# A decoder block with two recurrent mixers: another prologue and DeltaNet preparation, sigmoid gates inside the second recurrence, held joins, six steps a chunk

## The chip, the cores and the metric

The kernel runs on one core of a Trainium2 chip. The metric is the time of one execution in microseconds (us), the median of several runs. Engines: PE (TensorE, matrix products), DVE (VectorE), ACT (ScalarE), POOL (GpSimd), and SP, whose queue starts all DMA transfers of this kernel. Every engine works through its own list of instructions in order; semaphores tie them together.

## The reference

One block on x of 512 positions by 1024 channels, float32. A conditioning vector c gives shift, scale and gate by adaLN: a product of silu(c) with a 1024 x 6144 matrix. The normed and modulated x goes through one wide projection w_in to all inputs of two mixers and to two gates:

```python
h = rms_norm(x) * (1 + scale) + shift
q, k, v = split(silu(causal_conv4(h @ w_qkv)))         # gated DeltaNet, 8 heads of 64
y_gdn  = rms_norm(delta_rule(l2(q), l2(k), v, g, beta)) * silu(h @ w_z)
y_rwkv = group_norm(rwkv7_scan(r, decay, k, v, -kk, kk * a)) + bonus, times a gate
x = x + gate * ((sigmoid(ga) * (y_gdn @ w_bg) + sigmoid(gb) * (y_rwkv @ w_br)) @ w_out)
x = x + gate2 * conv_glu(rms_norm(x) * (1 + scale2) + shift2)      # 1024 -> 2 x 2816 -> 1024
```

Both recurrences run in 8 chunks of 64 positions; within a chunk a unit triangular 64 x 64 matrix per head is inverted.

## The kernel before, in words

**Layout.** All activations are kept as [channel, time], 128 channels by 512 positions a tile. A product tile of w_in takes 8 steps (k) of 3 matmuls: high part of the weights by high part of h (L187), high by low (L190), low by high (L191), all fp32r, 24 matmuls in a row into one of two PSUM banks (`mm`). The weights come as one 512 KB transfer into `raw`; ACT makes the high part `whi` (L146), DVE the low part `wlo` (L149). bg and br tiles have half the depth, 12 matmuls.

**Queue.** Products wait in a Python list; `fill(n)` emits n steps at a place in the program, so that PE has something to do between the dependent pieces of the recurrences; `need` emits until a product is done. When a product is begun, the weights of the next are requested. `late` adds transfers and sums of adaLN rows (`wada`, L210 and L211) ahead of a product. The framework's scheduler then orders each engine's instructions by what it thinks is ready, so the order isn't that of the program. Two things bind it: data, and `last["hold"]`, which puts every queue matmul behind the last `step` matmul that stands before it in the program (L188).

**Prologue (L333 to L371).** silu(c) is worked out on 128 x 8 numbers, spread to all partitions by two PE products. `first_tiles` does seven w_in tiles at once, k by k: two adaLN rows each summed on DVE (L202), A1 (L366), the normed h in high and low part (L305 to L307), the weights' low part on POOL for k from 1 on.

**DeltaNet preparation (L410 to L627).** Convolutions (one on ACT and POOL, L414 to L418, the others on DVE, L385), l2 norms (squares on POOL, L483), decay matrices (L505 on POOL, mask L512 on DVE), and a loop over chunks that makes `ginv`, the triangular matrices (L622 to L627).

**Solve (L541).** The 64 x 64 matrices are split in 32 x 32 blocks. They are written to DRAM (`lsc`, L548) and read back with another partition order (L551). DVE inverts the 32 x 32 blocks by 30 pairs of operations (L559, L561), ACT makes a transposed copy (`pr`, L565), and `tsc`, `usc` go through DRAM back. Then PE joins the blocks: for each half, 32 small matmuls (L582), a copy, 32 more (L592), a copy. It is a generator: the part after `yield` comes when it is run to its end, at L678 for DeltaNet (g) and at L850 for RWKV (r).

**Recurrences.** DeltaNet at L739 with 1, 1 and 3 steps of queue work (`more`) a chunk; RWKV at L856 with 3, 3 and 2 steps a chunk, `hold` on in both. Between them the pair matrices of RWKV (L807), its solve, the output norm of DeltaNet, silu(z), the eight bg products (into `ysc`) and transposes (`to_natural`). The order of queue products is GQ, LO, GV, RK and RR in turn, RV, Z, then gates GA (8) and GB (8), raw gates being copied to DRAM (`asc`, `bsc`).

**Merge (L936).** After the RWKV norm all of the queue is drained; the eight br products follow, each with two loads of gates, one of `ysc`, two sigmoids, a multiply on POOL (L944) and DVE work; then w_out, and the FFN.

Of the kernel before, what the change touches and what calls it, by code (L numbers as in the profile page):

```python
# [22 lines left out]
D = 1024  # L23
# [32 lines left out]
def body(ctx, tc, io, out, tap=lambda name, ap: None):  # L56
# [143 lines left out]
    def ada(j, w):  # L200
        sp.dma_start(w, io["w_ada"][j])
        i = dve.tensor_tensor_reduce(out=w, in0=w, in1=cond, scale=1.0, scalar=col("b_ada", j), op0=ALU.mult,  # L202
                                 op1=ALU.add, accum_out=mod[:, j:j + 1])
        if last["norm"] is not None:
            tc.add_manual_dep(i.ins, last["norm"].ins.name, after, reason="place")
# [20 lines left out]
    def product(label, src, xs_, evac, psum=mm, late=0, halves=False, spare=None):  # L226
# [3 lines left out]
        return dict(label=label, pieces=pieces, n=n, xs=xs_, evac=evac, psum=psum, late=late, halves=halves)  # L230

    def stream():
        while queue:
            it = queue.pop(0)
            for _ in range(min(it["late"], len(ada_rest))):
# [97 lines left out]
    cond = const.tile([128, D], F32, name="cond")  # L333
    table(EXP)
    fn(sc_, cc, AF.Exp, scale=-1.0)
    dve.tensor_scalar(sc_, sc_, 1.0, None, op0=ALU.add)
    dve.reciprocal(sc_, sc_)
    dve.tensor_tensor(sc_, sc_, cc, op=ALU.mult)
    pool.affine_select(out=diag.rearrange("p (k t) -> p k t", k=KT), in_=sc_.unsqueeze(2).broadcast_to([128, KT, 128]),
                       pattern=[[0, KT], [-1, 128]], base=0, channel_multiplier=1, compare_op=ALU.is_equal, fill=0.0)  # L340
    for u in range(2):
        p = pc()
        pe.matmul(p, one, diag[:, T * u:T * u + T], start=True, stop=True)
        act.copy(cond[:, T * u:T * u + T], p)
# [16 lines left out]

    def first_h(k):
        w = slot((2, 3, 8, 9, 12)[k]) if k < 5 else slot2((0, 2, 1)[k - 5])
        ada(8 + k, w[:, 0:D])
        ada(k, w[:, D:2 * D])
        dve.scalar_tensor_tensor(A1[:, k:k + 1], mod[:, 8 + k:9 + k], 1.0, col("norm1", k),  # L366
                                 op0=ALU.add, op1=ALU.mult)
# [42 lines left out]
    def gkq(a, j, side=False):  # L410
        def f(p):
            acc, w = tmp("sg" if side else "acc"), col("conv_gdn", 4 * (4 * (1 - a) + j), 4)
            if side:
                act.activation(acc, p, AF.Copy, scale=w[:, 3:4])  # L414
                for i in range(1, 4):
                    t = tmp("sp")
                    act.activation(t[:, :T - i], p[:, :T - i], AF.Copy, scale=w[:, 3 - i:4 - i])
                    pool.tensor_tensor(acc[:, i:], acc[:, i:], t[:, :T - i], op=ALU.add)  # L418
            else:
                conv(acc, p, w, 4)  # L420
# [82 lines left out]
    for b in range(4):  # L503
        gt = tmp("acc").rearrange("p (c h t) -> p c h t", c=2, h=4)
        pool.tensor_tensor(gt, gl[:, 2 * b:2 * b + 2, :].unsqueeze(3).broadcast_to([128, 2, 4, C]),  # L505
# [6 lines left out]
        dve.tensor_tensor(ex, ex, mask2[:, 1, :].unsqueeze(1).unsqueeze(1).broadcast_to([128, 2, 4, C]), op=ALU.mult)  # L512
# [28 lines left out]
    def solve(sv, name, work):  # L541
# [32 lines left out]
        yield  # L574
        for h in range(2):
# [3 lines left out]
            for i in range(16):  # L579
                for e in range(2):  # L580
                    lo_r, hi_r = slice(64 * e, 64 * e + 32), slice(64 * e + 32, 64 * e + 64)
                    pe.matmul(p[hi_r, i, :], sv[lo_r, 16 * h + i, 32:64], t1[lo_r, 16 * h + i, :],  # L582
# [6 lines left out]
            for i in range(16):  # L589
                for e in range(2):  # L590
                    lo_r, hi_r = slice(64 * e, 64 * e + 32), slice(64 * e + 32, 64 * e + 64)
                    pe.matmul(p[lo_r, i, :], ht[hi_r, i, :], sv[hi_r, 16 * h + i, 32:64],  # L592
                              start=True, stop=True)
# [23 lines left out]
    qs = [qe, ct4(gs[:, 2048:4096])]  # L617
    for c in range(NC):
# [5 lines left out]
        pool.tensor_tensor(qs[1][hs(1), :, tc_], qe[hs(1), :, tc_], eg[hs(1), :, tc_], op=ALU.mult)  # L624
# [19 lines left out]
    to_natural(gv, lambda e, c: gvn[hs(1 - e), c])  # L644
# [3 lines left out]
    zsc = dr.tile([4, 128, T], F32, name="zsc")  # L648
# [184 lines left out]
    for ct in range(4):  # L833
# [4 lines left out]
        split(ga_h[ct], ga_l[ct], sg)  # L838
    gx = list(zip(ga_h, ga_l))
# [9 lines left out]
    to_natural(kh, lambda e, c: kb[e][hs(1 - e), :, c * C:(c + 1) * C], True)  # L849
# [6 lines left out]
    for c in range(NC):  # L856
# [7 lines left out]
        fill(3)  # L864
# [5 lines left out]
        fill(3)  # L870
# [34 lines left out]
    table(EXP)  # L905
    rb_h, rb_l = quarter(slot(2, F32R)), quarter(slot(12, F32R))
# [22 lines left out]
    drain()  # L929
# [3 lines left out]
    mh = [hp.tile([128, T], F32R, name=f"hh{k}", tag=f"hh{k}") for k in range(KT)]  # L933
    ml = [hp.tile([128, T], F32R, name=f"hl{k}", tag=f"hl{k}") for k in range(KT)]

    def merge(n):  # L936
        def f(p):
            t, sa_t, sb_t, ya_t = tmp("acc"), tmp("sg"), tmp("sq"), tmp("rs")
            sp.dma_start(sa_t, asc[n])
            sp.dma_start(sb_t, bsc[n])  # L940
            sp.dma_start(ya_t, ysc[n])
            fn(sa_t, sa_t, AF.Sigmoid)
            fn(sb_t, sb_t, AF.Sigmoid)
            pool.tensor_tensor(ya_t, sa_t, ya_t, op=ALU.mult)  # L944
            dve.tensor_tensor(t, sb_t, p, op=ALU.mult)
            dve.tensor_tensor(t, t, ya_t, op=ALU.add)
            split(mh[n], ml[n], t)
        return f
# [211 lines left out]
```

## Time and profile before

| what | us |
|---|---|
| median of 3 runs (942.07 to 944.73) | 943.73 |
| the profiled execution, whole | 943.86 |
| its span of instructions | 942.2 |
| PE busy in the span | 887.0 |
| DVE / ACT / POOL busy | 548.0 / 413.5 / 150.0 |
| DeltaNet recurrence, first matmul | 208.66 |
| RWKV recurrence, first chunk's second step | 385.40 |
| FFN, from about | 565 |

How to read the profile: times are from the start of the span. A busy share is that of a stage; a row of the timeline gives start, length, engine, line, operation, output <- input and shape, and in brackets how long the engine had stood idle and what ended it. "xN" is the number of instructions in a row. PE matmuls overlap: a row's length is longer than the distance to the next.

### The profile page before, as it was taken

To read this page: it belongs to the slowest core of one execution; us is meant where nothing else is said; L and a number is where in the kernel's file an instruction comes from. 1 tells how busy PE (TensorE), PEld (TensorE's weight loads), DVE (VectorE), ACT (ScalarE), POOL (GpSimd) and SP (SyncE) were. 2 spreads that over 40 slices of the span, in tenths; PEclk is the share of its full clock that TensorE was granted. 3 is DMA by queue.
4 is the path that set the end of the run, shared out by engine and by line. 5 is a ranking of instruction groups with operands and counts; after the bars stand their busy time and mean duration, and the time that the engine had idled before them with its cause. 6 is when DMAs were issued, how large, how long until landed. Compare 5 with 4: busy or idle time off the path is not lost.

```text
span 942.2 us, 13945 instructions
## 1 busy us (share of the span) xinstructions
PE 887.0 (94%) x5463; PEld 690.9 (73%) x5463; DVE 548.0 (58%) x865; ACT 413.5 (44%) x663; POOL 150.0 (16%) x126
## 2 busy tenths in 40 slices
PE   5989889989989998899999999999999999999996
PEld 3666566876666776777667788888888888888885
DVE  7988988934976684245568537464544544322233
ACT  5247535355537658323465425343333333332231
POOL 2334630001542100011232230000000000010112
PEclk7999989989999999799999999999999999999998
DMA  9741232473234577444567543332232233533322
GB/s 322 261 151 46 67 101 68 144 170 102 58 90 112 197 232 202 142 146 153 186 200 256 181 139 91 106 106 96 90 103 99 89 105 97 173 101 100 96 89 90
DMA packets 81696, 126.26 MB, mean 134 GB/s; under 512 B 26237, under 2 KB 43005, under 8 KB 81566
## 3 DMA queue, kind: packets, MB, share of 16 engines
q1 hardware_dynamic: 81630, 125.36, 42.4%
q8 instruction: 43, 0.70, 0.3%
q14 instruction: 23, 0.19, 0.1%
HBM read 110.14 MB, written 14.68 MB: 132 GB/s over the span
## 4 chain that ended last, share of the span: by engine, by line
PE 70%; DVE 14%; ACT 7%; DMA 3%; issue 3%; POOL 2%; SPq 0%; DVEq 0%; ACTq 0%; POOLq 0%
PE ps_mm L187 19%; PE ps_mm L191 19%; PE ps_mm L190 19%; PE ps_pc L182 3%; DVE wlo L149 2%; ACT whi L146 1%; DVE slot L202 1%; ACT slot L607 1%; DMA wada<-in_w_ada 1%; DVE slotd L202 1%; DVE wada L211 1%; PE ps_pa L592 1%; ACT tmp_rs L94 1%; PE ps_pc L187 1%; PE ps_pa L622 1%
## 5 line engine op out<-in xcount | busy, mean ns | idle before, releaser
L187 PE MATMUL ps_mm<-hh,whi 128*128 128x512 f32 (+1 forms) x714 | 292.1, 410 | 8.5 <-ACT hh L306 3.5
L191 PE MATMUL ps_mm<-hh,wlo 128*128 128x512 f32 (+1 forms) x714 | 282.5, 396 | 4.7 <-POOL wlo L149 3.5
L190 PE MATMUL ps_mm<-hl,whi 128*128 128x512 f32 (+1 forms) x714 | 282.3, 395 | 1.5 <-DVE hl L307 1.5
L149 DVE TENSOR_TENSOR wlo<-raw,whi 128x1024 fp32r<-128x1024 f32 (+2 forms) x133 | 156.7, 1178 | 169.1 <-ACT whi L146 163.5
L146 ACT CAST whi<-raw 128x1024 fp32r<-128x1024 f32 (+2 forms) x140 | 136.9, 979 | 242.8 <-PE ps_mm L190 190.4
L187 PEld LDWEIGHTS ps_mm<-hh,whi 128*128 128x128 f32 x714 | 136.0, 191 | 47.6 <-issue 9.8
L191 PEld LDWEIGHTS ps_mm<-hh,wlo 128*128 128x128 f32 x714 | 136.6, 191 | 37.9 <-POOL wlo L149 5.2
L190 PEld LDWEIGHTS ps_mm<-hl,whi 128*128 128x128 f32 x714 | 136.7, 191 | 32.1 <-issue 3.6
L191 PE MATMUL ps_mm<-slot,wlo 128*128 128x512 f32 (+1 forms) x154 | 58.5, 380 | 1.7 <-DVE wlo L149 1.7
L187 PE MATMUL ps_mm<-slot,whi 128*128 128x512 f32 (+1 forms) x154 | 58.0, 379 | 0.0
L190 PE MATMUL ps_mm<-slot,whi 128*128 128x512 f32 (+1 forms) x122 | 45.4, 372 | 0.0
L968 POOL COPY tmp_rs<-tmp_sq 128x512 f32<-128x512 f32 x2 | 2.1, 1066 | 268.8 <-ACT tmp_sq L965 268.8
L211 DVE CUSTOM_DVE_ANT_0 wada<-wada,cond,cols 128x512 f32<-128x512 f32 x32 | 25.1, 785 | 26.5 <-DMA wada<-in_w_ada 26.3
L211 DVE CUSTOM_DVE_ANT_0 wada<-wada,cond,half 128x512 f32<-128x512 f32 x32 | 25.2, 787 | 21.7 <-DMA wada<-in_w_ada 21.6
L187 PE MATMUL ps_mm<-slotd,whi 128*128 128x512 f32 (+1 forms) x96 | 36.4, 379 | 0.0
L190 PE MATMUL ps_mm<-slotd,whi 128*128 128x512 f32 (+1 forms) x96 | 36.1, 376 | 0.0
L191 PE MATMUL ps_mm<-slotd,wlo 128*128 128x512 f32 (+1 forms) x96 | 36.1, 376 | 0.0
L970 POOL TENSOR_TENSOR tmp_rs<-tmp_rs,tmp_sq 128x512 f32<-128x512 f32 x12 | 19.5, 1624 | 103.8 <-ACT tmp_sq L965 103.8
L191 PEld LDWEIGHTS ps_mm<-slot,wlo 128*128 128x128 f32 x154 | 29.0, 188 | 9.1 <-DVE wlo L149 4.0
L1035 DVE TENSOR_TENSOR tmp_sg<-tmp_acc,ps_mm 128x512 f32<-128x512 f32 x20 | 13.8, 688 | 35.6 <-PE ps_mm L191 35.5
L385 DVE SCALAR_TENSOR_TENSOR tmp_acc<-ps_mm,cols,tmp_acc 128x511 f32<-128x511 f32 (+2 forms) x44 | 32.8, 745 | 0.7
L187 PEld LDWEIGHTS ps_mm<-slot,whi 128*128 128x128 f32 x154 | 28.9, 188 | 5.8 <-ACT whi L146 0.4
(279 smaller groups left out, 1336.0 us busy)
## 6 DMA issues: line engine op xcount, KB each, us to landing
raw<-in_w_in SPq DMA_DIRECT2D x40, 512.0 KB, 3.5
raw<-in_w_fi SPq DMA_DIRECT2D x37, 512.0 KB, 3.5
wada<-in_w_ada SPq DMA_DIRECT2D x64, 256.0 KB, 3.1
raw<-in_w_fo SPq DMA_DIRECT2D x16, 512.0 KB, 3.5
slot<-in_w_ada SPq DMA_DIRECT2D x10, 512.0 KB, 6.8
slot<-in_xT SPq DMA_DIRECT2D x16, 256.0 KB, 4.1
raw<-in_w_out SPq DMA_DIRECT2D x8, 512.0 KB, 3.7
raw<-in_w_in SPq DMA_DIRECT2D x8, 448.0 KB, 4.5
```

What stands on the lines that cost most here:

```text
L94: i = act.activation(*a, **k)
L146: i = act.copy(hi, src)
L149: j = eng.tensor_tensor(lo, src, hi.bitcast(F32), op=ALU.subtract)
L182: last["step"] = pe.matmul(*a, **k)
L187: i = pe.matmul(p, hi, xh, start=start, stop=False)
L190: pe.matmul(p, hi, xl, start=False, stop=False)
L191: pe.matmul(p, lo, xh, start=False, stop=stop)
L202: i = dve.tensor_tensor_reduce(out=w, in0=w, in1=cond, scale=1.0, scalar=col("b_ada", j), op0=ALU.mult, op1=ALU.add, accum_out=mod[:, j:j ...
L211: i = dve.tensor_tensor_reduce(out=w, in0=w, in1=cond[:, part], scale=1.0, scalar=half[:, j:j + 1] if u else col("b_ada", j), op0=ALU.mult ...
L385: dve.scalar_tensor_tensor(acc[:, i:], p[:, :T - i], w[:, taps - 1 - i:taps - i], acc[:, i:], op0=ALU.mult, op1=ALU.add)
L970: pool.tensor_tensor(sums[0], sums[0], sq, op=ALU.add)
L1035: dve.tensor_tensor(t, accs[j], p, op=ALU.mult)
```

## The change

It has six parts.

1. *Conditioning vector.* c comes as a 128 x 1024 broadcast from the host (512 KB), in the queue between the fourth and fifth tile of x; ACT takes its SiLU. The PE broadcast goes.
2. *Prologue.* Loads are requested one or two k ahead; the weights' low part is on DVE for all k; A1 on ACT.
3. *Preparation.* The one convolution goes to DVE; squares of the l2 norm go to ACT (L492 after), decay product (L514) to DVE, the mask to POOL as eight `affine_select`; `qs[1]` is one DVE operation ahead of the chunk loop; two fill steps a norm instead of one; copies of two transposes on ACT. The four Z products stand ahead of GV in the queue.
4. *Held joins.* Matmuls of the joins are `step`s and `hold` is on while they are emitted.
5. *Gates.* From ahead of the bg products ACT has the sigmoid table; a gate product is evacuated by sigmoid, GA multiplied by its y (fetched from DRAM). GB 6 and 7 are left for the branch stage, one ahead of br 0 and one ahead of br 3, and stay in SBUF; loads for the merge are requested one product ahead; `late` is 3 for GA, 4 for GB, 0 for br.
6. *RWKV recurrence.* Two, two and two queue steps a chunk.

```diff
-    sp.dma_start(cc, io["c"])
     for k in range(KT):
         sp.dma_start(xT(k), io["xT"][k])
+        if k == 3:
+            sp.dma_start(cond, io["c"])
...
-            split(hi[:, :128 * count], lo[:, :128 * count], raw[:, :128 * count], side if k else dve, () if k else behind)
+            split(hi[:, :128 * count], lo[:, :128 * count], raw[:, :128 * count], dve, () if k else behind)
...
+    table(SILU)
+    fn(cond, cond, AF.Silu)
     table(EXP)
-    fn(sc_, cc, AF.Exp, scale=-1.0)
...
-        dve.scalar_tensor_tensor(A1[:, k:k + 1], mod[:, 8 + k:9 + k], 1.0, col("norm1", k),
-                                 op0=ALU.add, op1=ALU.mult)
+        act.activation(A1[:, k:k + 1], mod[:, 8 + k:9 + k], AF.Identity, scale=col("norm1", k), bias=col("norm1", k))
...
+    for j in range(4):
+        inproj(T_Z + j, spill(zsc[j]))
     for j in range(4):
         inproj(T_GV + j, lambda p, j=j: conv(gv[:, j], p, col("conv_gdn", 4 * (8 + j), 4), 4))
...
-        pool.tensor_tensor(sq, dst, dst, op=ALU.mult)
+        act.activation(sq, dst, AF.Square)
...
-        pool.tensor_tensor(gt, gl[:, 2 * b:2 * b + 2, :].unsqueeze(3).broadcast_to([128, 2, 4, C]),
+        dve.tensor_tensor(gt, gl[:, 2 * b:2 * b + 2, :].unsqueeze(3).broadcast_to([128, 2, 4, C]),
...
-        dve.tensor_tensor(ex, ex, mask2[:, 1, :].unsqueeze(1).unsqueeze(1).broadcast_to([128, 2, 4, C]), op=ALU.mult)
+        for e in range(2):
+            d = ex[64 * e:64 * e + 64]
+            pool.affine_select(out=d, in_=d, pattern=[[0, 2], [0, 4], [1, C]], base=0, channel_multiplier=-1,
+                               compare_op=ALU.is_ge, fill=0.0)
...
+        held, last["hold"] = last["hold"], True
         for h in range(2):
...
-                    pe.matmul(p[hi_r, i, :], sv[lo_r, 16 * h + i, 32:64], t1[lo_r, 16 * h + i, :],
+                    step(p[hi_r, i, :], sv[lo_r, 16 * h + i, 32:64], t1[lo_r, 16 * h + i, :],
...
+    dve.tensor_tensor(qs[1][hs(1)], qe[hs(1)], eg[hs(1)], op=ALU.mult)
...
-        pool.tensor_tensor(qs[1][hs(1), :, tc_], qe[hs(1), :, tc_], eg[hs(1), :, tc_], op=ALU.mult)
...
+    def gate(n, dst):
+        def f(p):
+            o = tmp("sp")
+            if sig_in[0]:
+                fn(o, p, AF.Sigmoid)
+            else:
+                act.copy(o, p)
+                raw_gate.add(n)
+            if ("y", n) in fetched:
+                dve.tensor_tensor(o, o, fetched.pop(("y", n)), op=ALU.mult)
+                with_y.add(n)
+            sp.dma_start(dst, o)
+        return f
...
-        fill(3)
+        fill(2)
...
-    drain()
+    need(T_GB + KT - 3)
...
-            pool.tensor_tensor(ya_t, sa_t, ya_t, op=ALU.mult)
...
+        if n in (0, 3):
+            g = KT - 2 + n // 3
+            queue.append(product(T_GB + g, io["w_in"][T_GB + g], hx, last_gate(g), ahead=1))
-        queue.append(product(("br", n), io["w_br"][n], bx, merge(n), late=2))
+        queue.append(product(("br", n), io["w_br"][n], bx, merge(n), begin=merge_in(n), ahead=1))
```

How instructions move, on PE at the joins of the first solve. Before, from the last matmuls of the product `ps_mm_1652` (one of RK and RR; five whole ones of these stand right ahead of it) to the recurrence's first matmuls (`ps_pc_1684`); `slot10` and `slotd2` hold the solve's blocks:

```order
L187 MATMUL ps_mm_1652<-hh7_113,whi_1615 128x512
L190 MATMUL ps_mm_1652<-hl7_121,whi_1615 128x512
L191 MATMUL ps_mm_1652<-hh7_113,wlo_1616 128x512
L582 MATMUL ps_pa_1298<-slot10_943,slotd2_830 32x32 x31
L592 MATMUL ps_pa_1342<-slotd2_830,tmp_sg_1299 32x32
L582 MATMUL ps_pa_1390<-slot10_943,slotd2_830 32x32 x32
L592 MATMUL ps_pa_1432<-slotd2_830,tmp_sg_1391 32x32
L592 MATMUL ps_pa_1342<-slotd2_830,tmp_sg_1299 32x32 x31
L592 MATMUL ps_pa_1432<-slotd2_830,tmp_sg_1391 32x32 x31
L182 MATMUL ps_pc_1684<-slot8_1206,slotd2_830 64x64 x8
L690 MATMUL ps_pa_1697<-slot11_473 128x512
L187 MATMUL ps_mm_1706<-hh0_106,whi_1648 128x512
```

The joins follow the products and run without queue matmuls between them. The same place after, where `ps_mm_1376` is the first of the eight RK and RR products and the joins have L181, the line of `step`:

```order
L713 MATMUL ps_pa_1398<-slot11_461 128x512
L713 MATMUL ps_pa_1404<-slot11_461 128x512
L181 MATMUL ps_pa_1410<-slot10_957,slotd2_851 32x32 x32
L186 MATMUL ps_mm_1376<-hh6_110,whi_1366 128x512
L189 MATMUL ps_mm_1376<-hl6_118,whi_1366 128x512
L190 MATMUL ps_mm_1376<-hh6_110,wlo_1367 128x512
L186 MATMUL ps_mm_1376<-hh7_111,whi_1366 128x512
L189 MATMUL ps_mm_1376<-hl7_119,whi_1366 128x512
L190 MATMUL ps_mm_1376<-hh7_111,wlo_1367 128x512
L181 MATMUL ps_pa_1454<-slotd2_851,tmp_sg_1411 32x32 x32
L186 MATMUL ps_mm_1493<-hh0_104,whi_1372 128x512
L189 MATMUL ps_mm_1493<-hl0_112,whi_1372 128x512
```

The joins now come behind three quarters of the first RK product, two queue steps stand in each gap, and the rest of the RK and RR products follow behind the last join.

On SP at the first solve's write and read. Before:

```order
L548 DMA lsc_g_936<-slotd2_830 32x32x32 x4
L157 DMA raw_1252<-in_w_in 128x1024
L157 DMA raw_1258<-in_w_in 128x1024
L551 DMA slot10_943<-lsc_g_936 128x1024
L210 DMA wada_3039<-in_w_ada 128x512
```

After, with the spills of Z 0 to Z 3 (`zsc`):

```order
L409 DMA zsc_467<-tmp_sp_848 128x512
L560 DMA lsc_g_950<-slotd2_851 32x32x32 x4
L409 DMA zsc_467<-tmp_sp_1108 128x512
L409 DMA zsc_467<-tmp_sp_1142 128x512
L156 DMA raw_1145<-in_w_in 128x1024
L563 DMA slot10_957<-lsc_g_950 128x1024
L409 DMA zsc_467<-tmp_sp_1176 128x512
```

Two spills and one weight load stand between write and read where there were two weight loads.

More of the change, by code (lines that the diff above doesn't have):

```diff
@@ L224, in body, with product @@
     queue, done = [], set()
-    def product(label, src, xs_, evac, psum=mm, late=0, halves=False, spare=None):
+    def product(label, src, xs_, evac, psum=mm, late=0, halves=False, spare=None, begin=None, ahead=0):
         n = src.shape[-1] // 128
@@ L229, in product @@
                   for k0 in range(0, n, 8)]
-        return dict(label=label, pieces=pieces, n=n, xs=xs_, evac=evac, psum=psum, late=late, halves=halves)
+        return dict(label=label, pieces=pieces, n=n, xs=xs_, evac=evac, psum=psum, late=late, halves=halves, begin=begin, ahead=ahead)
     def stream():
@@ L234, in stream @@
             it = queue.pop(0)
+            for nx in [it] + queue[:it["ahead"]]:
+                if nx["begin"] is not None:
+                    nx["begin"]()
+                    nx["begin"] = None
             for _ in range(min(it["late"], len(ada_rest))):
@@ L408, in body, with gkq @@
     pool.memset(wt[64:65], 1.0)
-    def gkq(a, j, side=False):
+    def gkq(a, j):
         def f(p):
[L412 to L420, printed above, removed]
+            acc, w = tmp("acc"), col("conv_gdn", 4 * (4 * (1 - a) + j), 4)
+            conv(acc, p, w, 4)
             fn(kq[:, a, j], acc, AF.Silu)
         return f
-    inproj(T_GQ + 2, gkq(1, 2, True), pa)
+    inproj(T_GQ + 2, gkq(1, 2), pa)
     inproj(T_GQ + 3, gkq(1, 3))
@@ L597, in solve @@
                 act.mul(sv[lo_r, i_, 32:64], p[lo_r], -1.0)
+        last["hold"] = held
     def to_natural(src, place, quiet=False):
@@ L661, in body, with fetch, f @@
         shift_in(T_RV + j, rv_[:, j], 8 + j)
-    for j in range(4):
-        inproj(T_Z + j, spill(zsc[j]))
+    sig_in = [False]
+    raw_gate, with_y = set(), set()
+    fetched = {}
+    def fetch(label, tag, src):
+        def f():
+            fetched[label] = tmp(tag)
+            sp.dma_start(fetched[label], src)
+        return f
[11 more added lines that the diff above has]
+            sp.dma_start(dst, o)
+        return f
     for n in range(KT):
-        inproj(T_GA + n, spill(asc[n]))
-    for n in range(KT):
-        inproj(T_GB + n, spill(bsc[n]))
+        inproj(T_GA + n, gate(("a", n), asc[n]),
+               begin=lambda n=n: fetch(("y", ("a", n)), "rs", ysc[n])() if ("bg", n) in done else None)
+    for n in range(KT - 2):
+        inproj(T_GB + n, gate(("b", n), bsc[n]))
     lw = ct4(slot(12))
@@ L838, in body @@
         split(ga_h[ct], ga_l[ct], sg)
+    table(SIG)
+    sig_in[0] = True
     gx = list(zip(ga_h, ga_l))
@@ L928, in body, with last_gate, f, merge_in @@
         fill(2)
[L929 removed]
+    need(T_GB + KT - 3)
     table(SIG)
[L933 to L934 removed]
+    mh = quarter(slot(8, F32R)) + quarter(slot(10, F32R))
+    mls = slot2(0, F32R)
+    ml = [mls[:, T * k:T * k + T] for k in range(KT)]
+    gates, gate_slot = {}, quarter(slot(11))
+    def last_gate(n):
+        def f(p):
+            gates[n] = gate_slot[len(gates)]
+            fn(gates[n], p, AF.Sigmoid)
+        return f
     def merge(n):
         def f(p):
[L938 to L943, printed above, removed]
[L944 to L947 removed]
+            t = tmp("acc")
+            if n in gates:
+                sb_t = gates[n]
+            else:
+                sb_t = fetched[("b", n)]
+                if ("b", n) in raw_gate:
+                    fn(sb_t, sb_t, AF.Sigmoid)
+            dve.tensor_tensor(t, sb_t, p, op=ALU.mult)
+            sa_t = fetched[("a", n)]
+            if ("a", n) in raw_gate:
+                fn(sa_t, sa_t, AF.Sigmoid)
+            if ("a", n) not in with_y:
+                dve.tensor_tensor(sa_t, sa_t, fetched[("y", n)], op=ALU.mult)
+            dve.tensor_tensor(t, t, sa_t, op=ALU.add)
+            split(mh[n], ml[n], t)
+        return f
+    def merge_in(n):
+        def f():
+            fetch(("a", n), "sg", asc[n])()
+            if n < KT - 2:
+                fetch(("b", n), "sq", bsc[n])()
+            if ("a", n) not in with_y:
+                fetch(("y", n), "rs", ysc[n])()
         return f
```

73 lines of the change are left out of this document (39 added, 34 removed).

## The prediction

> **What bounds the kernel now.** I read the page first, then the table by stage, then the rows where TensorE (PE) stands still.
>
> The page: busy time of each engine, and the engines' shares of the chain that ended last.
>
> ```profile
> span 942.2 us, 13945 instructions
> PE 887.0 (94%) x5463; PEld 690.9 (73%) x5463; DVE 548.0 (58%) x865; ACT 413.5 (44%) x663; POOL 150.0 (16%) x126
> PE 70%; DVE 14%; ACT 7%; DMA 3%; issue 3%; POOL 2%; SPq 0%; DVEq 0%; ACTq 0%; POOLq 0%
> ```
>
> PE is the bound, and what can be won or lost is the time in which it has nothing to do. The table by stage (stage, length, busy time of PE, its weight loads, DVE, ACT, POOL, granted PE clock, DMA share, GB/s) shows where that is:
>
> ```profile
> 0.00:64.50 64.50, 48.60 (x172) 33.83 (x173) 53.50 (x71) 25.77 (x36) 19.71 (x22) 0.92 0.76 256
> 64.50:121.80 57.30, 52.13 (x309) 35.91 (x308) 51.87 (x86) 34.35 (x59) 27.82 (x25) 0.97 0.19 61
> 121.80:201.30 79.50, 73.89 (x315) 57.49 (x313) 63.31 (x133) 33.85 (x51) 9.74 (x7) 0.96 0.48 129
> 208.40:297.20 88.80, 82.24 (x919) 56.64 (x915) 60.87 (x104) 47.95 (x100) 27.31 (x26) 0.94 0.28 84
> 297.20:371.70 74.50, 70.47 (x313) 52.67 (x307) 51.68 (x118) 52.43 (x103) 8.76 (x5) 0.98 0.70 204
> 385.20:457.00 71.80, 71.37 (x789) 54.48 (x784) 34.89 (x65) 22.71 (x42) 7.45 (x7) 0.97 0.47 154
> 457.00:520.00 63.00, 60.87 (x234) 42.38 (x233) 45.06 (x72) 37.61 (x60) 20.22 (x14) 1.00 0.65 212
> 520.00:565.00 45.00, 43.11 (x193) 35.54 (x192) 19.34 (x21) 16.97 (x21) 12.41 (x9) 0.96 0.46 153
> 565.00:930.00 365.00, 364.33 (x1690) 304.85 (x1689) 161.70 (x192) 129.87 (x171) 13.86 (x11) 1.00 0.32 101
> ```
>
> From 565 PE is full (364 of 365 us) and the change leaves that code as it was: the FFN is a constant. Ahead of it the stages are the prologue (to 64.5), the DeltaNet preparation (to 121.8, with DVE busy 52 of 57), the first solve beside queue products (to 201), the two recurrences and the second solve. All queue products are the same in number before and after. So I compare the programs at landmarks: the **balance** is the time at a landmark, later or earlier than before, minus the queue matmuls already done beyond those of before, at the pitch of a dense stretch, here 30 us:
>
> ```profile
> L191 PE MATMUL ps_mm<-hh,wlo 128*128 128x512 f32 x45 | 17.9, 398 | 0.0
> L187 PE MATMUL ps_mm<-hh,whi 128*128 128x512 f32 x45 | 17.5, 389 | 0.0
> L190 PE MATMUL ps_mm<-hl,whi 128*128 128x512 f32 x44 | 17.1, 389 | 0.0
> ```
>
> 134 starts in 30 us: 0.224 us each, 5.4 us for a product of 24. The span is 942.2 us and this execution's time 943.86, 0.13 above the median 943.73, so a difference in the balance goes straight onto either.
>
> **Part 1, prologue and preparation (to the last ginv product).** DVE and POOL rows (start, length):
>
> ```profile
> 17.04 1.28 DVE L202 CUSTOM_DVE_ANT_0 slot<-slot,cond,cols 128x1024 f32<-128x1024 f32 x1
> 19.45 2.04 DVE L366 SCALAR_TENSOR_TENSOR A<-mod,cols 128x1 f32<-128x1 f32 x1
> 29.92 3.19 DVE L202 CUSTOM_DVE_ANT_0 slot<-slot,cond,cols 128x1024 f32<-128x1024 f32 x1
> 19.36 2.12 POOL L149 TENSOR_TENSOR wlo<-raw,whi 128x896 fp32r<-128x896 f32 x1 [8.96 <-ACT whi L146]
> 58.38 2.08 POOL L149 TENSOR_TENSOR wlo<-raw,whi 128x896 fp32r<-128x896 f32 x1 [2.50 <-ACT whi L146]
> 15.37 1.09 DVE L149 TENSOR_TENSOR wlo<-raw,whi 128x896 fp32r<-128x896 f32 x1
> 14.54 0.75 DVE L305 SCALAR_TENSOR_TENSOR tmp_acc<-slot,A,tmp_rs 128x512 f32<-128x512 f32 x1 [0.48 <-ACT tmp_rs L94]
> ```
>
> Each k's low part took 2.1 us on POOL, and the DVE operation beside it was stretched by 1.9 (a 128x1 operation to 2.04, 1.28 to 3.19). The seven POOL rows stand 39.0 us apart from first to last, 6.5 a piece. After, DVE does per k two ada sums (2 x 1.28), two 0.75 passes and the split's 1.09, together 5.1 or a little less, and PE's 21 matmuls are 4.7: six steps save some 8. Against that, the 512 KB broadcast of c stands in the queue ahead of the ada rows, and SiLU of 1024 columns with one table more ahead of rstd: I take 3 us (bounds 1.5 and 5). Net -5, from 0 to -7.
>
> The Trainium skill, "GPSIMD Engine Reference", its table's row on SBUF interfaces, says that POOL shares them with VectorE and contends with instructions of two SBUF inputs. The 1.28 to 3.19 agrees; by that rule the new POOL masks would stretch DVE's two-input work again, and the term below would lose 2 to 4 us.
>
> ```profile
> L488 DVE SCALAR_TENSOR_TENSOR slotd<-slotd,tmp_rs 128x512 f32<-128x512 f32 x8 | 7.1, 893 | 0.8 <-ACT s L94 0.8
> L512 DVE TENSOR_TENSOR tmp_sg<-tmp_sg,cons 128x512 f32<-128x512 f32 x4 | 5.2, 1290 | 0.0
> 120.90 0.86 DVE L627 TENSOR_TENSOR slotd<-ps_pa,slotd 64x256 f32<-64x256 f32 x2
> ```
>
> Preparation: DVE gains three conv passes and four gate multiplies (7 at the 0.7 of such a pass), the 64x2048 multiply (four passes' length, 2.8) and three ada halves (an L202 sum of 1.28 is two of them, 2), about 10; it loses four masks (5.2) and the stretching by POOL (8 x 0.2 on L488, and I take 3 for the others). Net 0, from -4 to +4. So the last ginv product moves from 121.8 to about 117, and at that point the order holds 22 queue matmuls more (294 against 272): balance -5 - 4.9 = **-10**.
>
> **Part 2, the first solve and its held joins.** Here I expect the loss. Rows of DVE and ACT, the end of the solve, and of PE:
>
> ```profile
> 147.40 1.13 DVE L552 TENSOR_SCALAR slot<-slot 128x1024 f32<-128x1024 f32 x1
> 189.31 2.12 ACT pr L565
> 201.53 1.19 PE L582 MATMUL ps_pa<-slot,slotd 32*32 32x32 f32 x62 [1.03 <-DMA slot<-tsc_g]
> 205.27 3.45 PE L592 MATMUL ps_pa<-slotd,tmp_sg 32*32 32x32 f32 x126 [0.68 <-ACT tmp_sg L587]
> 208.66 1.12 PE L182 MATMUL ps_pc<-slot,slotd 64*64 64x64 f32 x16
> ```
>
> Before, 80 us pass from the last ginv multiply (121.8) to the joins (201.5), PE waits only 1.03 us there, because the scheduler had pulled five RK and RR products in front of the joins. After, the hold puts these behind. Between ginv and joins PE has about 180 queue matmuls (40.4), eight groups of transposes and the four w2 products (as long as before, some 7) and one short wait where GV 0's weights stand behind Z 3's copy on ACT (2.5): 50 us.
>
> The chain hardly shortens. The read of lsc now stands behind the spills of Z 1 and Z 2 and a weight load, and DVE's first solve step behind a split that waits for Z 3: about 20 us after ginv instead of 25.6. From there (147.4) to ACT's copy (189.3) DVE took 41.9; it has the same 60 steps, twelve conv passes instead of eight, two ada halves more, a split and eight small copies less: 44. Copy, transposing DMAs and landing were 12.2. Together 77, so PE stands idle some 27 us. Then the joins (four half joins, some 4.6, around 30 queue matmuls, 6.8) and the six products that had been in front (144 matmuls, 32.3): recurrence at 77 + 44 = 121 after ginv, before 86.9. That is 34 later with 74 matmuls more (16.6): **+17**, from +7 (ten us less idle) to +25. The balance at the recurrence is +7; nothing in it changes up to 297.
>
> **Part 3, the second solve.**
>
> ```profile
> 318.21 1.12 DVE L552 TENSOR_SCALAR slot<-slot 128x1024 f32<-128x1024 f32 x1
> 360.30 2.11 ACT L565 COPY pr<-slot 128x1024 f32<-128x1024 f32 x1
> 376.54 1.19 PE L582 MATMUL ps_pa<-slot,slotd 32*32 32x32 f32 x62
> 385.40 0.91 PE L182 MATMUL ps_pc<-cz,slotd 64*64 64x64 f32 x12
> ```
>
> With Z done, four silu products, two ada halves and three splits fewer stand among the solve steps: 42 becomes 36, and copy to joins stays 14 (the copies of bh and kh queue behind it on ACT). Joins at 70 after 297 instead of 79, but only 183 queue matmuls (41) and 9 of others are there to cover it: 20 idle. The recurrence's second step, then, is about 8 us earlier with 54 matmuls (12.1) fewer: **+4**, from -1 to +9.
>
> **Part 4, clock.** Two rows of the table by windows, the first right after the first joins, the second across the second:
>
> ```profile
> 205.40:215.60 10.20, 10.20 (x180) 7.65 (x179) 2.78 (x5) 5.76 (x11) 0.62 (x1) 0.51 0.24 80
> 379.50:389.60 10.10, 8.02 (x157) 6.97 (x150) 1.25 (x2) 5.41 (x9) 0.00 (x0) 0.51 0.31 111
> ```
>
> The clock is half for 10 us after the joins already. After a wait of 20 to 27 us those 10 us cover the queue matmuls within the held joins (30 of them, at most 6.7 us more each time): I take **+3** for both, from 0 to +10. The Trainium skill, "TensorE: Matmul & The Clock Gate", the part on the HAM clock gate, gives about 3.4 us of busy time until the clock is full again; by that the term is +1 or +2, but the rows here show 10.
>
> **Part 5, recurrence and gates.** Chunk rows on ACT:
>
> ```profile
> 402.81 0.38 ACT L863 COPY cz<-ps_pc 128x256 f32<-128x256 f32 x1 [1.89 <-PE ps_pc L182]
> 405.64 0.38 ACT L868 ACTIVATE slot<-ps_pc 64x256 f32<-64x256 f32 x1 [2.45 <-DVE half L211]
> ```
>
> Two steps (1.34) cover a copy of 0.38 and its way; the six matmuls taken out come later, at the same price. The new DVE multiply by y and ada halves can hold the small DVE operations: **+1.5**, from 0 to +5. In the branch stage PE lacks 4 us in 457 to 565; products by POOL, the ada sums and the late loads go from it: **-3**, from -4 to 0. Sigmoid at evacuation costs ACT the same copy.
>
> Sum: -10 + 17 + 4 + 3 + 1.5 - 3 = +12.5, so 943.9 + 12.5 = 956.
>
> **Rivals.** (a) *Faster: the front's gain outlasts the solve.* If DVE, freed from POOL, ends ginv at 113 (balance -14) and the wait before the joins is 17 and not 27 (+7), with +1 for the second solve, no clock and -4 at the branches, it gives -10: 934. It decides at a chain from ginv to joins of some 67 us. For it: DVE is the bound of that stage and POOL's stretching is plain. Against it: 41.9 us of DVE steps that nothing here removes. 0.32. (b) *The holds at their worst*: full +25, +9 and +6 of clock give 970 and more. 0.08. (c) *No change*: gains and holds cancel, or the added Z covers the joins as RK and RR did. 943.9. 0.13. (d) My forecast, 945 to 967: 0.47.
>
> **How the numbers follow.** A difference of 0.3% (2.8 us) is about what a measurement of this kernel tells from none. The likeliest case gives 956; the range takes in (c) and most of (a) and ends at the bound of (b): 931 to 970. Faster 0.32 (a), within 0.13 (c), slower 0.55 (b and d).
>
> **What would show it.** Right: last ginv multiply near 117; PE idle over 20 us just ahead of the first join, released by a DMA of usc or tsc; again 15 or more before the second joins; half clock in the 10 us behind; chunks of 7.7 to 8 us instead of 9.0 (72 us for eight); no POOL wait at the merges. Wrong: joins that start when PE's own products end, ginv before 113, or a prologue not shorter.

## The result, and the profile after

| | before | after |
|---|---|---|
| median, us (4 runs each) | 944.23 (942.07 to 944.96) | 950.61 (949.40 to 950.79) |
| ratio after / before, 95% interval | | 1.0063 (1.0042 to 1.0085) |
| profiled execution, us | 943.86 | 949.40 |

The change makes the kernel 0.63% slower, 6.4 us of medians; the spans of the two profiled executions differ by 5.5 us. First the page after: span, busy time of the engines, the PE clock in 40 slices, and the engines' shares of the chain that ended last.

```profile
span 947.7 us, 13866 instructions
PE 878.3 (93%) x5459; PEld 687.6 (73%) x5459; DVE 536.4 (57%) x866; ACT 416.5 (44%) x672; POOL 94.4 (10%) x91
PEclk9999999679999999999999999999999999999998
PE 67%; DVE 12%; DMA 9%; issue 5%; ACT 4%; POOL 1%; SPq 1%; DVEq 0%; ACTq 0%; POOLq 0%
```

POOL is busy 56 us less, DVE 12 us less, and the span is longer all the same. The chain's DMA share went from 3% to 9%, and the clock has a dip at its eighth and ninth slice, 166 to 213 us. The table by stage of after (columns as before) shows the same place:

```profile
120.10:190.50 70.40, 53.05 (x211) 38.29 (x209) 48.61 (x112) 30.67 (x56) 2.43 (x3) 0.85 0.55 154
160.00:172.50 12.50, 8.80 (x44) 6.51 (x43) 12.22 (x30) 7.39 (x15) 0.00 (x0) 1.00 0.40 130
172.50:187.50 15.00, 6.78 (x10) 1.92 (x8) 7.69 (x27) 7.67 (x14) 0.00 (x0) 0.51 0.60 168
190.50:200.00 9.50, 9.46 (x140) 7.26 (x142) 3.31 (x6) 4.79 (x7) 0.00 (x0) 0.50 0.20 56
200.00:239.00 39.00, 39.00 (x290) 32.31 (x290) 17.17 (x30) 12.26 (x16) 0.00 (x0) 1.00 0.46 142
323.70:393.60 69.90, 56.62 (x257) 41.13 (x257) 51.62 (x117) 46.69 (x92) 9.29 (x5) 0.98 0.69 196
469.20:570.70 101.50, 100.76 (x427) 77.18 (x425) 56.03 (x75) 47.99 (x69) 21.23 (x15) 1.00 0.46 149
```

From the last ginv product to the first join (first line) PE is busy 53 of 70 us; in the 15 us of the third line it starts ten matmuls, and the granted clock falls from 1.00 to 0.51. The rows of PE there (start, length, in brackets the idle time ahead and what ended it):

```profile
172.17 6.96 PE L713 MATMUL ps_pa<-slot 65*128 65x512 f32 x8 [0.92 <-issue]
187.17 0.28 PE L181 MATMUL ps_pa<-slot,slotd 32*32 32x32 f32 x2 [8.04 <-issue]
190.54 1.91 PE L181 MATMUL ps_pa<-slot,slotd 32*32 32x32 f32 x62 [3.09 <-DMA slot<-tsc_g]
...
193.40 0.63 PE L190 MATMUL ps_mm<-hh,wlo 128*128 128x512 f32 x1
193.83 0.63 PE L186 MATMUL ps_mm<-hh,whi 128*128 128x512 f32 x1
...
199.95 1.29 PE L181 MATMUL ps_pa<-slot,slotd 32*32 32x32 f32 x64
```

From 172 on PE has nothing but the eight matmuls of the w2 products (L713). Then it stands idle for 8.0 us, for which the profile names no releaser, and for 3.1 us until a DMA of `tsc` lands. In the kernel before with the hold (second experiment) the same two matmuls (the row at 187.17 here) do wait for the DMA of `tsc`. The queue matmuls within the joins (193.40 to 193.83) follow at 0.43 us each instead of 0.224.

The balance of after at each landmark (time against before, less 0.224 us for each queue matmul done more), counted from the two traces, beside the prediction's running sum. The counts include the 168 matmuls of the first seven tiles. Each trace is one execution, and executions of one kernel differ by several us (last section), so a balance is good to a few us only.

| landmark | before: us, matmuls | after | balance | predicted |
|---|---|---|---|---|
| last ginv product | 121.8, 276 | 120.1, 299 | -6.8 | -10 |
| first dense join | 201.5, 552 | 190.5, 474 | +6.5 | |
| DeltaNet recurrence | 208.7, 552 | 239.5, 648 | +9.3 | +7 |
| output norm | 297.6, 669 | 323.7, 765 | +4.6 | +7 |
| RWKV, second step | 385.4, 933 | 408.4, 978 | +12.9 | +14 |
| RWKV norm | 455.7, 1116 | 469.2, 1119 | +12.8 | +15.5 |
| FFN | 565.4, 1512 | 570.7, 1512 | +5.3 | +12.5 |

### The profile page after: what moved, and what is told of

It is laid out like the page before. It is cut to its first block, busy times and chain, and to the rows that moved or that the text cites. A ratio compares the mean times of both kernels' runs of the same rounds, so it can differ in the third digit from the quotient of the medians.

```text
span 947.7 us, 13866 instructions
## 1 busy us (share of the span) xinstructions
PE 878.3 (93%) x5459; PEld 687.6 (73%) x5459; DVE 536.4 (57%) x866; ACT 416.5 (44%) x672; POOL 94.4 (10%) x91
## 4 chain that ended last, share of the span: by engine, by line
PE 67%; DVE 12%; DMA 9%; issue 5%; ACT 4%; POOL 1%; SPq 1%; DVEq 0%; ACTq 0%; POOLq 0%
PE ps_mm L186 18%; PE ps_mm L189 17%; PE ps_mm L190 17%; DMA wada<-in_w_ada 6%; DVE wlo L148 3%; PE ps_pc L181 2%; DVE wada L209 2%; PE ps_pa L181 1%; PE ps_pc L186 1%; PE ps_pc L190 1%; PE ps_pc L189 1%; PE ps_pa L186 1%; PE ps_pa L189 1%; DMA raw<-in_w_in 1%; PE ps_pa L190 1%
## 5 line engine op out<-in xcount | busy, mean ns | idle before, releaser
L186 PE MATMUL ps_mm<-hh,whi 128*128 128x512 f32 (+1 forms) x642 | 264.9, 413 | 8.5 <-ACT hh L308 3.4
L190 PE MATMUL ps_mm<-hh,wlo 128*128 128x512 f32 (+1 forms) x642 | 254.7, 398 | 0.6 <-DVE wlo L148 0.5
L189 PE MATMUL ps_mm<-hl,whi 128*128 128x512 f32 (+1 forms) x642 | 254.1, 396 | 0.0
L186 PEld LDWEIGHTS ps_mm<-hh,whi 128*128 128x128 f32 x642 | 122.0, 190 | 44.5 <-issue 7.3
L190 PEld LDWEIGHTS ps_mm<-hh,wlo 128*128 128x128 f32 x642 | 122.2, 190 | 30.2 <-issue 3.1
L189 PEld LDWEIGHTS ps_mm<-hl,whi 128*128 128x128 f32 x642 | 122.5, 191 | 26.2 <-issue 3.3
L186 PE MATMUL ps_mm<-slot,whi 128*128 128x512 f32 (+1 forms) x226 | 85.6, 379 | 4.6 <-ACT tmp_sp L94 4.6
L190 PE MATMUL ps_mm<-slot,wlo 128*128 128x512 f32 (+1 forms) x226 | 84.7, 375 | 0.0
L189 PE MATMUL ps_mm<-slotd,whi 128*128 128x512 f32 (+1 forms) x168 | 62.4, 371 | 0.0
L189 PE MATMUL ps_mm<-slot,whi 128*128 128x512 f32 (+1 forms) x122 | 45.3, 372 | 0.0
L186 PE MATMUL ps_mm<-slotd,whi 128*128 128x512 f32 (+1 forms) x96 | 36.4, 380 | 0.0
L189 PEld LDWEIGHTS ps_mm<-slotd,whi 128*128 128x128 f32 x168 | 31.6, 188 | 5.7
```

The source lines that it names most:

```text
L186: i = pe.matmul(p, hi, xh, start=start, stop=False)
L189: pe.matmul(p, hi, xl, start=False, stop=False)
L190: pe.matmul(p, lo, xh, start=False, stop=stop)
```

## The experiments

Each ratio is to runs of the kernel before on the same chip (medians there 945.36, 945.66 and 945.40).

**Undoing the hold.** In after, the two lines that set and clear it go, and the joins are plain matmuls:

```diff
-        held, last["hold"] = last["hold"], True
...
-                    step(p[hi_r, i, :], sv[lo_r, 16 * h + i, 32:64], t1[lo_r, 16 * h + i, :],
+                    pe.matmul(p[hi_r, i, :], sv[lo_r, 16 * h + i, 32:64], t1[lo_r, 16 * h + i, :],
...
-        last["hold"] = held
```

> The changed kernel with the hold taken from the joins of both solves, all else as changed. Theory (the hold keeps queue products behind the first joins and PE stands idle): in PE's order 562 instead of 474 queue matmuls now stand ahead of the first join, so the 12 us of idle time ahead of it and the half clock behind it go; about 14 us faster than the changed kernel, 935 to 940, faster than before. Rival (the wait for the solve's chain costs the same wherever the products stand, since they are only moved): 949 to 952.

Measured: 936.81, ratio 0.9909 (0.9877 to 0.9941): faster than before. The table by stage of this kernel, ginv to joins and the second solve:

```profile
121.20:204.40 83.20, 79.24 (x338) 60.69 (x337) 56.13 (x120) 38.33 (x66) 2.36 (x3) 0.98 0.55 158
309.60:385.90 76.30, 65.54 (x289) 48.93 (x289) 56.62 (x122) 48.99 (x96) 8.07 (x5) 0.93 0.62 181
```

The joins start 13 us later after ginv than with the hold (83.2 against 70.4), but 600 queue matmuls are done by then and not 474: PE was busy 79 of the 83 us. The balance at the first join is -7.9 against +6.5, 14.4 apart. Further on the two traces are 17.2 us apart at the recurrence, 14.0 at the output norm and 10.8 at the FFN; this kernel's profiled execution, 938.65, is the slowest of its six. By the ratios, 1.0063 and 0.9909, the two kernels are 14.6 us apart. So the hold's price is paid at the first solve, and the second adds nothing that shows.

**The hold alone, on before.** The same lines, added to the kernel before.

> The kernel before with the held joins alone. Theory: 378 instead of 541 queue matmuls ahead of the first join; joins at the same time, 174 matmuls (39 us) behind the first of them instead of 11: 30 to 38 us slower than before, 975 to 985. Rival (holds only reorder): 942 to 948.

Measured: 970.21, ratio 1.0265 (1.0219 to 1.0310): the direction as expected, the size smaller, 25 us where 30 to 38 were expected. The profiled execution, 975.33, is the slowest of its four. The stage from ginv to the joins and the ten us behind, then PE's wait:

```profile
122.30:193.00 70.70, 38.03 (x143) 26.71 (x141) 51.23 (x118) 21.05 (x35) 9.73 (x7) 0.71 0.40 106
193.00:203.00 10.00, 10.00 (x161) 7.80 (x162) 3.31 (x6) 4.79 (x7) 0.00 (x0) 0.50 0.18 57
```

```profile
189.39 0.28 PE L182 MATMUL ps_pa<-slot,slotd 32*32 32x32 f32 x2 [21.35 <-DMA slot<-tsc_g]
```

Only 378 queue matmuls stand ahead of the joins here, 96 fewer than in after (21.5 us); the price grows from 14 to 25 us. The chain from ginv to the joins is 70.7 long, as in after (70.4), though neither Z nor the preparation changed: in both, PE waits for the solve, so some 70 us is the length of the solve itself.

**Hold kept, cover restored.** In after, the RK and RR products are drained ahead of the joins instead of behind them:

```diff
+    need(T_RR + 3)
     for _ in gsolve:
         pass
-    need(T_RR + 3)
```

> The changed kernel with the RK and RR products finished ahead of the first solve's held joins instead of behind them; both joins still held. Theory (not the hold but what it leaves behind the joins is the cost): 600 queue matmuls ahead of the first join as without a hold; 934 to 940. Rival (held joins cost by themselves, by the clock or by their fills): 945 or more.

Measured: 938.48, ratio 0.9932 (0.9909 to 0.9954). 600 queue matmuls are again ahead of the first join, as without the hold, and the loss is gone. So what costs is not that the joins are `step`s, but which products they keep back.

**Z ahead or not.** First in before, Z alone ahead of GV; then after without the hold and with Z back behind RV:

```diff
+    for j in range(4):
+        inproj(T_Z + j, spill(zsc[j]))
     for j in range(4):
         inproj(T_GV + j, lambda p, j=j: conv(gv[:, j], p, col("conv_gdn", 4 * (8 + j), 4), 4))
...
-    for j in range(4):
-        inproj(T_Z + j, spill(zsc[j]))
```

> The kernel before with the four Z products ahead of GV alone. Theory (Z only moves cover from the second solve to the first, which had enough of it): 3 to 8 us slower than before, 947 to 952, with idle time ahead of the second joins. Rival (Z fills idle time in preparation and first solve): 936 to 941.

Measured: 945.07, ratio 1.0001 (0.9978 to 1.0023): no change, where the theory wanted a loss. Its balance is -8.4 at the first joins and -0.9 at the second. The second solve (from the output norm to the second joins) of before, then of this kernel:

```profile
297.40:376.30 78.90, 74.87 (x340) 55.98 (x338) 52.72 (x118) 55.43 (x109) 8.76 (x5) 0.98 0.68 199
```

```profile
310.80:386.40 75.60, 65.04 (x290) 46.73 (x290) 51.48 (x114) 52.27 (x104) 9.17 (x5) 0.98 0.63 181
```

Fifty matmuls fewer are left for that stretch, it shortens by only 3.3 us, and PE stands idle 10.6 instead of 4.0. What Z covers in one solve it no longer covers in the other.

> As the first, and the four Z products back behind RV. Theory: 544 queue matmuls ahead of the first join, enough cover as before; Z again covers the second solve (916 ahead of its joins instead of 961 at a later time); 933 to 940, within 4 us of the first. Rival (the early Z products are what gains time): slower than the first by 5 us or more.

Measured: 934.82, ratio 0.9894 (0.9862 to 0.9925), 1.4 us below the first experiment, less than the intervals can tell. From the output norm to RWKV's second step the balance now loses 3.4 us, where the first experiment lost 8.8.

**The rest, part by part, in before.** The prologue (parts 1 and 2 of the change); the preparation (part 3 without Z); the gates and the merge (part 5, eight steps a chunk); the last with six (part 6).

```diff
+            sp.dma_start(cond, io["c"])
...
+    fn(cond, cond, AF.Silu)
```

> The kernel before with the changed prologue alone (broadcast c, SiLU, loads ahead, low parts on DVE, A1 on ACT). Theory from the two traces (the first matmul of the 8th tile starts 6.3 us earlier, 58.5 instead of 64.8, but the last ginv multiply ends only 1.6 us earlier): the gain is partly lost in the preparation; 4 to 6 us faster than before, 939 to 942. Rival (all of it arrives): 7 us or more faster. Rival (none arrives, DVE sets the preparation): within 2 us of before.

Measured: 938.24, ratio 0.9929 (0.9907 to 0.9951). 7.1 per thousand is 6.7 us: above the theory's bound and just below the rival's.

```diff
-        pool.tensor_tensor(sq, dst, dst, op=ALU.mult)
+        act.activation(sq, dst, AF.Square)
...
```

> The kernel before with the changed preparation alone (convolution on DVE, squares on ACT, masks on POOL, one multiply ahead of the chunk loop, two fill steps a norm; Z stays late, joins not held). Theory (DVE gets some 10 us of work and loses some 10 of work and stretching; PE does 22 queue matmuls more by the end of it, of which only part is a gain): within 3 us of before, 941 to 947. Rival (POOL's stretching was the bound): 5 us or more faster. Rival (DVE is the bound and gets more): 3 us or more slower.

Measured: 942.35, ratio 0.9981 (0.9954 to 1.0008), no difference that can be told. The last ginv operations of the prologue alone and of the preparation alone:

```profile
115.12 0.86 DVE L636 TENSOR_TENSOR slotd<-ps_pa,slotd 64x256 f32<-64x256 f32 x2
```

```profile
129.13 0.86 DVE L623 TENSOR_TENSOR slotd<-ps_pa,slotd 64x256 f32<-64x256 f32 x2
```

Against 120.90 before, the prologue brings ginv forward by 5.8 us; the preparation delays it by 8.2, with 32 queue matmuls (7.2 us) more done by then. It swaps one for the other.

```diff
+                fn(o, p, AF.Sigmoid)
...
+                dve.tensor_tensor(o, o, fetched.pop(("y", n)), op=ALU.mult)
```

> The kernel before with the changed gates and merge alone (sigmoid at evacuation, y multiplied in the recurrence, two GB products in the branch stage, loads ahead, no POOL multiply, ada sums moved forward); eight steps a chunk. Theory (the idle time of PE between 495 and 565, 3 waits of 5.1 us together, goes as it did in the changed kernel): 4 to 6 us faster than before, 938 to 941. Rival (the ada sums and gate multiplies hold the recurrence): no faster than before.

Measured: 943.65, ratio 0.9986 (0.9963 to 1.0010): the gain expected isn't there. By the balance it is, but only from the RWKV norm on (+5.6 to -0.7, 6.3 us); ahead of it, from the output norm (0.0) to there, 5.6 us are lost.

```diff
-        fill(3)
+        fill(2)
...
-        fill(3)
+        fill(2)
```

> As the one before, with 2, 2 and 2 steps a chunk. Theory (PE is dense in a chunk with 8 steps; with 6 the two steps are only done later, and the chunk comes out of its own chain now and then): 0 to 3 us slower than with eight steps. Rival (the chunk gets shorter by more than its steps, since the queue was what held it): 2 us or more faster than with eight.

Measured: 946.37, ratio 1.0014 (0.9987 to 1.0041): six steps instead of eight are worth nothing, or a little loss. Added up, the parts alone (prologue -6.7, preparation -1.8, gates with six steps +1.3, Z +0.1) make -7.1 us; the kernel with all of them and no hold, the first experiment, measured -8.6. So the hold is what turns a gain into a loss.

**Together, without the hold.** Prologue and gates in before:

> The kernel before with the changed prologue and the changed gates, eight steps, nothing held, preparation and Z as before. Theory (prologue 0.7% and gates 0.1% add, preparation brings 0.2% at most): 936 to 940. Rival (the parts only gain together): 942 or more.

Measured: 936.14, ratio 0.9903 (0.9875 to 0.9931); the two alone sum to 0.9915. Next the kernel with neither hold nor early Z, with eight steps a chunk:

> Not held, Z late, and eight steps a chunk again in the RWKV recurrence. Theory (six or eight steps only move work): within 2 us of the same with six, 932 to 938. Rival (six steps leave the chunk to its own chain): 3 us or more faster than with six.

Measured: 933.22, ratio 0.9888 (0.9860 to 0.9916), as with six. Last the same kernel with six steps and the hold in the RWKV solve alone (the edit of the hold against after):

```diff
-        held, last["hold"] = last["hold"], True
+        held, last["hold"] = last["hold"], name == "r"
```

> Z late, hold in the second solve's joins alone. Theory from the traces (second solve: the changed kernel lost 8 to 9 us there, and so did the one that is not held with Z early, so the hold is no cost there): within 2 us of Z late not held, 933 to 938. Rival (a held join stalls there too): 942 or more.

Measured: 931.50, ratio 0.9869 (0.9841 to 0.9896), the best median of all, 1.3% below before. Second solve without the hold, and with it:

```profile
290.50:370.70 80.20, 73.63 (x335) 54.53 (x335) 57.96 (x126) 52.55 (x100) 7.87 (x5) 1.00 0.66 198
```

```profile
289.60:364.00 74.40, 66.54 (x307) 49.78 (x309) 53.64 (x121) 50.33 (x97) 8.83 (x5) 0.98 0.71 210
```

Here the hold keeps back 30 matmuls (6.7 us) and the joins come 5.8 us sooner; PE's idle time is 7.9 against 6.6 us. The joins come sooner by nearly as much as the matmuls kept back take, so that nothing is lost. The 95% intervals of this kernel and of the one without any hold overlap: a gain of the hold here is possible, not shown.

## Why the prediction was right, and where it wasn't

The direction was right, and so was the mechanism at the first solve: held joins without cover, a wait that ends with a DMA of `tsc`, half clock behind it. The size was half (6.4 for 12.5). The gains in the DeltaNet recurrence and the branches were 9.2 us larger together than booked, the RWKV recurrence was 1.7 us better, the front and the second solve (with the clock's +3) 4.5 us worse. The range, 931 to 970, took in no change and most of a faster kernel, so the time alone would prove little; what bears the prediction out is the loss at the first solve, which the experiments put on the hold.

**Prologue, -5: right.** The first `ps_mm` matmul of the queue is the same point of both programs; before, then after:

```profile
70.40 0.39 PE L187 MATMUL ps_mm<-hh,whi 128*128 128x512 f32 x1
```

```profile
64.28 0.39 PE L186 MATMUL ps_mm<-hh,whi 128*128 128x512 f32 x1
```

6.1 us, within 0 to 7; alone it gave 5.8 at ginv.

**Preparation, 0, and 22 matmuls as well: mis-sized.** From that point to the last ginv product, in the table by stage before and after:

```profile
70.40:121.80 51.40, 46.23 (x283) 31.02 (x282) 46.20 (x78) 30.52 (x54) 25.95 (x24) 0.97 0.17 53
```

```profile
64.30:120.10 55.80, 51.32 (x310) 35.70 (x308) 46.47 (x88) 35.15 (x62) 8.17 (x10) 0.97 0.20 67
```

It takes 4.4 us longer, so ginv ends at 120.1 and not at 117. The 23 queue matmuls more are there, but so is their time (23 x 0.224 = 5.2). PE is busy for 90 and 92% of the stage, DVE for 90 and 83%: PE paces it as much as DVE does. The term "ginv at 117" and the "-4.9" for matmuls therefore counted one gain twice. Two groups of DVE there, after (mean ns behind the busy time), then single rows of them and the row of POOL's first two masks:

```profile
L497 DVE SCALAR_TENSOR_TENSOR slotd<-slotd,tmp_rs 128x512 f32<-128x512 f32 x8 | 5.9, 739 | 0.8 <-ACT tmp_rs L94 0.8
L514 DVE TENSOR_TENSOR tmp_acc<-gl,cons 128x512 f32<-128x512 f32 x4 | 3.6, 910 | 0.0
```

```profile
91.31 0.68 DVE L514 TENSOR_TENSOR tmp_acc<-gl,cons 128x512 f32<-128x512 f32 x1
96.11 0.68 DVE L497 SCALAR_TENSOR_TENSOR slotd<-slotd,tmp_rs 128x512 f32<-128x512 f32 x1
96.90 2.24 POOL L523 TENSOR_SCALAR_AFFINE_SELECT tmp_sg<-tmp_sg 64x512 f32<-64x512 f32 x2 [45.07 <-ACT tmp_sg L94]
97.48 1.13 DVE L497 SCALAR_TENSOR_TENSOR slotd<-slotd,tmp_rs 128x512 f32<-128x512 f32 x1
99.79 2.20 DVE L514 TENSOR_TENSOR tmp_acc<-gl,cons 128x512 f32<-128x512 f32 x2
104.51 0.69 DVE L525 TENSOR_TENSOR slotd<-tmp_sg,beta 128x512 f32<-128x512 f32 x1 [1.25 <-POOL tmp_sg L523]
```

The stretched operation of before (893 ns) fell to 739, so POOL's leaving did free DVE. Of the rows after, those away from the masks take 0.68 us each. Beside the masks (96.90 to 106.87) one L497 takes 1.13, two L514 take 2.20 together, and one ada half takes 1.24 instead of 0.74: some 1.8 us of stretching, and DVE waits another 1.8 us for the masks themselves (L525). The Trainium skill ("GPSIMD Engine Reference", the table's row on SBUF interfaces) has POOL contend with VectorE instructions of two SBUF inputs, by which the prediction put 2 to 4 us on the new masks. The trace agrees: stretching and waits come to 3.6 us.

**First solve, +17: right as a sum; its two parts missed by 7 and 5 us and cancel.** The balance moves by 16.1. Rows of DVE and, behind them, of ACT:

```profile
119.28 0.86 DVE L641 TENSOR_TENSOR slotd<-ps_pa,slotd 64x256 f32<-64x256 f32 x2
...
137.21 1.23 DVE L148 TENSOR_TENSOR wlo<-raw,whi 128x1024 fp32r<-128x1024 f32 x1 [9.22 <-ACT whi L145]
138.35 1.08 DVE L564 TENSOR_SCALAR slot<-slot 128x1024 f32<-128x1024 f32 x1
```

```profile
179.66 1.92 ACT L577 COPY pr<-slot 128x1024 f32<-128x1024 f32 x1
```

DVE's first step comes 18.2 us after ginv (predicted 20), behind the split that waits 9.22 us for ACT; 41.3 to the copy (44), 10.9 to the joins (12): 70.4, where the prediction wrote 77 (its own terms make 76). Counted as the prediction did (175 matmuls at 0.224, 7 us of others, 2.5 of a wait), PE is without work for 22 us (27). So the chain ended nearer to the 67 us of rival (a) than to the forecast. From join to recurrence it took 49.0 for 44, with 9.7 us at half clock in it, and that made up for most of the chain. The sign asked for over 20 us of idle time just ahead of the first join; 8.0 and 3.1 us stand there, of 17 us idle in the whole stage.

**Nothing in the DeltaNet recurrence: wrong, -4.7.** Before, 10.6 us of the recurrence ran at half clock, 7.2 at its start and 3.4 from 267 on (by the granted clock of the trace); after, none did, because the half clock lies in the wait and the joins. Across all 14 traces the move of the balance through this recurrence follows the time at half clock in it (correlation 0.93): -4.7 us with none (after), -1.9 with 3.4 us (before with the hold), 0 with 10.6 (before), +3.2 with 17.0 (the preparation alone). What part 4 booked as a pure loss (+3) was for the larger part moved.

The clock at the first joins: 0.51 already in the wait, 0.50 for 9.5 us behind the first dense join, then 1.00; in the kernel before with the hold again 0.50 for 10 us. So the prediction's 10 us hold there. An estimate by the Trainium skill's 3.4 us ("TensorE: Matmul & The Clock Gate", the HAM clock gate) has it end at 194; the trace differs and decides. At the second joins of after it is the other way round, the half clock lasts only 3.4 us, with PE busy:

```profile
394.80:398.20 3.40, 3.40 (x30) 2.38 (x32) 0.87 (x3) 1.53 (x3) 0.00 (x0) 0.51 0.97 365
```

**Second solve, +4: mis-sized, and by another cause.** It is +8.3, where +4 and part of the clock's +3 were booked. The joins come 69.9 us after the output norm (70 predicted), with 13.3 us idle (20). The 70 is partly luck: the prediction took 14 us from copy to joins, but its rows (360.30 and 376.54) have 16.2, which makes 73; in after that piece took 12.9. To those joins the balance loses 9.1 in after, 8.7 without the hold, 7.4 with Z alone moved, and 1.9 with neither. It is Z's being gone, not the hold; with Z back the hold there cost nothing. Nor is it the wait for the solve that the prediction expected ahead of the joins. The longest wait of the stage, and the one at the joins, after:

```profile
347.28 0.79 PE L186 MATMUL ps_mm<-slot,whi 128*128 128x512 f32 x1 [4.63 <-ACT tmp_sp L94]
393.59 1.20 PE L181 MATMUL ps_pa<-slot,slotd 32*32 32x32 f32 x64 [0.87 <-ACT slot L621]
```

PE reaches the first bg product while ACT is still behind, and waits 4.6 us there; without the hold it waits 4.7 us at the same place, with Z alone moved 3.8 (for DVE's low part of the same input), with Z back and no hold not at all. All other waits that the profile lists for this stage end with ACT too, and none with a DMA of the solve. The prediction named the missing cover, but as part of the held joins and at another place.

**RWKV recurrence +1.5, branches -3: the first at the lower end of its bounds (-0.2 for 0 to +5), the second too small and outside them (-7.5 for -4 to 0).** The chunks come 7.7 to 8.8 us apart, about as predicted. Branches, before:

```profile
455.50:565.20 109.70, 105.20 (x430) 78.50 (x428) 65.65 (x94) 54.58 (x81) 34.08 (x23) 0.98 0.58 188
```

PE lacked 4.5 us of this stage; after, 0.7 of 101.5 (last line of the table by stage of after), at clock 1.00. The balance moves by 7.5: 3.8 for the gap, some 2.2 for the clock (0.02 of 110 us), and 1.5 that no row here explains. POOL no longer waits at the merges. In the nine kernels with the new gates the balance falls by 4.2 to 7.5 us in this stage; in the other four besides before it moves between -3.5 and +3.9.

**The rivals.** (a), faster because the front's gain outlasts the solve, fell by its own point: it asked for a chain of 67 us and got 70.4, for a front of -14 and got -6.8 (without the hold the kernel is faster, 936.8). (b), the holds at their worst (970), came in the kernel before, where no Z stood ahead. (c), the early Z covering the joins as RK and RR did, fell with 474 queue matmuls ahead of the first join, where before had 552.

**Left open.** Why the kernels with the new gates lose time between output norm and RWKV norm: 5.6 us alone in before, 6.0 with neither hold nor early Z, 2.8 with the new prologue only, 2.2 with the hold in the second solve. Six steps or eight don't explain it, and the gates may not either: the preparation alone, with the old gates, loses 2.0 us there, and before with the hold 2.8. And which of the preparation's new operations takes its time: the double count is read from the table, and its pieces weren't tried one by one.

## What to carry to other kernels

A wait bound by its own chain is only as cheap as the independent work that stands ahead of it: before ordering products behind a dependent step, count what is left to cover the step's latency, here 175 matmuls (39 us) against a chain of 70 us, and try the hold at each place alone (it cost 14 us at one solve and nothing that shows at the other). Work moved to cover one gap is taken from another: follow the balance to the next gap before booking a gain. Where PE is busy for nine tenths of a stage, don't count both an earlier end and the products done by then.

## What the hardware showed that was not expected

Before, the half clock began with PE busy, 4 us behind the start of the joins; after, it began ahead of them, in the stretch with ten matmuls in 15 us, and lasted 9.5 us into dense work, with queue matmuls at 0.43 us instead of 0.224. What sets its start wasn't tried. In all 14 traces the stretches at half clock (the one at the very end left out) are 3.4 us long or whole multiples of it: of 68, 35 are one such step and 21 are three; the longest, 44.4 us, is in the kernel before with the hold (158.7 to 203.1), the next, 27.3 us, in after (172.9 to 200.2).

The kernel before spread from 938.5 to 950.9 us in 35 runs on one chip, wider than the 0.3% counted on: differences of 2 to 3 us between these kernels are not told apart by six runs. The time goes with the mean clock that an execution was granted: 938.5 us at 0.986, 950.9 us at 0.968 (correlation over the 35 runs -0.73). So the time at half clock differs from one execution to the next.
